# A macaron block in fp32: both feed-forward parts as seven products of halves, in an up phase and a down phase

## The chip, the cores and the metric

The kernel runs on one core of a Trainium2 chip. The metric is the device time of one execution in microseconds. TensorE (PE) does the matrix products and the transposes, VectorE (DVE) and ScalarE (ACT) the element-wise work, GpSimd (POOL) a few row operations, and the SP queue issues nearly all DMAs. Every engine works through its own list of instructions in a fixed order; an instruction that waits holds back all that stand behind it on its engine.

## The reference

All in float32, one sequence of 1024 tokens, model width 1024, feed-forward width 2816.

```python
def swiglu(x, w1, w3, w2):
    return (jax.nn.silu(x @ w1) * (x @ w3)) @ w2
...
        x = layer_norm(ALPHA * x + 0.5 * swiglu(x, ffn1_w1[i], ffn1_w3[i], ffn1_w2[i]),
                       ln1_g[i], ln1_b[i])
        proj = x @ w_in[i]
        q_lat, kv_lat, k_rope, u, g_a, g_b = jnp.split(proj, SPLIT_POINTS, axis=-1)
        y_a = mla_attention(q_lat, kv_lat, k_rope, q_norm_g[i], kv_norm_g[i],
                            w_uq[i], w_uk[i], w_uv[i]) @ w_o_attn[i]
...
        merged = jax.nn.sigmoid(g_a) * y_a + jax.nn.sigmoid(g_b) * y_b
```

After that come the out projection and its layer norm, a second feed-forward part of the same form with its layer norm, and a gated projection of a side input. A second block, a mixer whose norm is modulated by a row computed with `mod_w`, ends the program; the change does not touch its products.

## The kernel before

Each float32 operand is held as the exact sum of a high and a low part (type `fp32r`), so each product of tiles is three matmuls of 128 x 128 by 128 x 512 (`mm3`, line L100). The parts are made by `split`: ScalarE casts the high part (L79), VectorE subtracts it (L80).

`ffn` (L169 to L219) goes over the 22 feature tiles of 128 in blocks of two, the last two blocks of three. For each feature tile and token half it forms the two up products (24 matmuls each), then `silu` (L201), the product (L202) and the split into `hh` and `hl`. Then the block's part of the down product goes into the eight token tiles `acc`, which lie in SBUF all along; VectorE adds each PSUM result to them (L215 to L219). Weights come from HBM once, block by block, and nothing of the hidden layer leaves the chip. In matmuls, one feed-forward part has 22 x 2 x 2 x 24 = 2112 up and 22 x 16 x 3 = 1056 down.

Two pieces of work that need no result of the feed-forward part run beside it. Beside the first it is `s5_tables`, a generator whose pieces are emitted by `tick`: the tables of the state-space branch, complex products on VectorE in a scratch tile `arena`, with transposes on TensorE and round trips through DRAM (`sd`). Beside the second it is `modulation` (multiply-adds L1214, 70 instructions of VectorE). The order of instructions on each engine is fixed when the program is built. Buffers come from pools; a pool's space is given to the next pool once its last reader is done, and the first writer into it waits for that.

After the first feed-forward part come `latents`, `u_cols`, and sixteen `gates` columns (48 matmuls a column each); between them stand eight `s5_batch` (chunk scans that read a batch's tables, `s5b_tab`), one for every two gates. After a feed-forward part the layer norm of its token tiles runs as a chain of small instructions (`nq`, L106 to L131); POOL applies gain and bias to the rows (`affine`, L1027 and L1028).

## Time and profile before

| | before |
|---|---|
| time, median of 3 runs | 3319.93 us (3316.15 to 3321.29) |
| span of the profiled execution | 3318.2 us |
| granted TensorE clock, mean | 0.992 |
| PE busy | 3244.3 us (98%) |
| DVE busy | 2046.8 us (62%) |
| ACT busy | 1103.9 us (33%) |
| POOL busy | 147.9 us (4%) |
| moved by DMA | 293.51 MB, mean 88 GB/s |

The profiled execution lies inside the range of the three runs, so its microseconds can be compared with the median as they are. The first feed-forward part lies at 0 to about 780 us, latents, gates and attention at about 800 to 1480 us, the second feed-forward part at about 1660 to 2400 us.

### The profile page before, as it was taken

To read this page: it belongs to the slowest core of one execution; us is meant where nothing else is said; L and a number is where in the kernel's file an instruction comes from. 1 tells how busy PE (TensorE), PEld (TensorE's weight loads), DVE (VectorE), ACT (ScalarE), POOL (GpSimd) and SP (SyncE) were. 2 spreads that over 40 slices of the span, in tenths; PEclk is the share of its full clock that TensorE was granted. 3 is DMA by queue.
4 is the path that set the end of the run, shared out by engine and by line. 5 is a ranking of instruction groups with operands and counts; after the bars stand their busy time and mean duration, and the time that the engine had idled before them with its cause. 6 is when DMAs were issued, how large, how long until landed. Compare 5 with 4: busy or idle time off the path is not lost.

```text
span 3318.2 us, 38245 instructions
## 1 busy us (share of the span) xinstructions
PE 3244.3 (98%) x15029; PEld 2638.8 (80%) x15029; DVE 2046.8 (62%) x3446; ACT 1103.9 (33%) x1579; POOL 147.9 (4%) x86
## 2 busy tenths in 40 slices
PE   9999999997999999999999999999989999999998
PEld 7878878876888888877778888888868888888786
DVE  6755555447236577776664543332498498899668
ACT  3111111123221266652331111122144456555443
POOL 0000000002200000000230000000040000000000
PEclk9999999998999999999999999999989999999999
DMA  4222222221434300034322232111123222322545
GB/s 131 61 69 73 71 79 63 73 80 45 138 122 140 114 16 13 14 127 145 132 80 76 74 99 69 45 57 51 45 89 118 91 76 76 97 85 72 195 156 182
DMA packets 291971, 293.51 MB, mean 88 GB/s; under 512 B 42581, under 2 KB 228366, under 8 KB 290766
## 3 DMA queue, kind: packets, MB, share of 16 engines
q1 hardware_dynamic: 291790, 291.06, 27.9%
q8 instruction: 118, 1.93, 0.2%
q14 instruction: 63, 0.52, 0.0%
HBM read 234.90 MB, written 56.10 MB: 88 GB/s over the span
## 4 chain that ended last, share of the span: by engine, by line
PE 91%; DVE 5%; DMA 2%; ACT 2%; issue 1%; SPq 0%; DVEq 0%; ACTq 0%
PE up L100 56%; PE dn L100 19%; PE up L1018 10%; PE tr L858 1%; PE dn L875 1%; DVE x L80 1%; DVE wl L80 1%; PE tr L143 1%; DVE sm L841 0%; PE up L544 0%; DMA gb<-gd 0%; DMA y<-yd 0%; DMA raw<-in_ffn_w_dram 0%; DVE nq L113 0%; ACT e L845 0%
## 5 line engine op out<-in xcount | busy, mean ns | idle before, releaser
L100 PE MATMUL up<-x,wh 128*128 128x512 f32 x5088 | 1640.1, 397 | 28.6 <-DVE x L80 22.5
L100 PEld LDWEIGHTS up<-x,wh 128*128 128x128 f32 x5088 | 955.5, 188 | 262.7 <-DVE x L80 25.9
L100 PE MATMUL up<-x,wl 128*128 128x512 f32 x2544 | 1006.8, 396 | 0.4 <-DVE wl L80 0.3
L100 PEld LDWEIGHTS up<-x,wl 128*128 128x128 f32 x2544 | 478.6, 188 | 114.0 <-DVE wl L80 1.4
L80 DVE TENSOR_TENSOR wl<-raw,wh 128x1024 fp32r<-128x1024 f32 (+3 forms) x251 | 316.9, 1264 | 273.5 <-ACT wh L79 271.0
L79 ACT CAST wh<-raw 128x1024 fp32r<-128x1024 f32 (+3 forms) x251 | 254.0, 1014 | 454.3 <-PE up L100 290.9
L1018 PE MATMUL up<-wh,x 128*128 128x512 f32 x1024 | 322.3, 396 | 0.0
L100 PE MATMUL dn<-w2l,hh 128*128 128x512 f32 x640 | 253.6, 397 | 0.0
L100 PE MATMUL dn<-w2h,hh 128*128 128x512 f32 x640 | 251.1, 393 | 0.0
L100 PE MATMUL dn<-w2h,hl 128*128 128x512 f32 x640 | 250.8, 392 | 0.0
L215 DVE SCALAR_TENSOR_TENSOR acc<-dn,acc 128x512 f32<-128x512 f32 x160 | 109.7, 689 | 212.0 <-PE dn L100 211.8
L201 ACT ACTIVATE s<-up 128x512 f32<-128x512 f32 x88 | 52.5, 597 | 564.4 <-PE up L100 564.2
L1018 PEld LDWEIGHTS up<-wh,x 128*128 128x128 f32 x1024 | 193.5, 190 | 41.4 <-issue 0.2
L1018 PE MATMUL up<-wl,x 128*128 128x512 f32 x512 | 202.9, 398 | 4.7 <-ACT xf L1769 2.4
L219 DVE TENSOR_TENSOR acc<-acc,dn 128x512 f32<-128x512 f32 x144 | 98.5, 684 | 134.0 <-PE dn L100 133.2
L202 DVE TENSOR_TENSOR s<-s,up 128x512 f32<-128x512 f32 x88 | 60.3, 685 | 186.1 <-ACT s L201 186.1
L1690 DVE SCALAR_TENSOR_TENSOR cv<-u,kc,cv 128x1024 f32<-128x1024 f32 x120 | 153.2, 1276 | 1.2
L100 PEld LDWEIGHTS dn<-w2l,hh 128*128 128x128 f32 x640 | 120.2, 188 | 28.8 <-issue 0.5
L100 PEld LDWEIGHTS dn<-w2h,hh 128*128 128x128 f32 x640 | 120.1, 188 | 27.7
L100 PEld LDWEIGHTS dn<-w2h,hl 128*128 128x128 f32 x640 | 120.2, 188 | 27.0
L1018 PEld LDWEIGHTS up<-wl,x 128*128 128x128 f32 x512 | 97.1, 190 | 29.7 <-DVE wl L80 3.1
L100 PE MATMUL up<-k,qh 128*128 128x512 f32 x256 | 92.9, 405 | 2.3 <-ACT e L845 2.3
(515 smaller groups left out, 4016.3 us busy)
## 6 DMA issues: line engine op xcount, KB each, us to landing
raw<-in_ffn_w_dram SPq DMA_DIRECT2D x132, 512.0 KB
raw<-in_w_in_dram SPq DMA_DIRECT2D x69, 512.0 KB
raw<-in_w_out_dram SPq DMA_DIRECT2D x44, 512.0 KB
s5b_tab<-sd SPq DMA_DIRECT2D x8, 1792.0 KB
sd<-arena SPq DMA_DIRECT2D x48, 256.0 KB
raw<-in_mod_w_dram SPq DMA_DIRECT2D x24, 512.0 KB
gd<-g SPq DMA_DIRECT2D x16, 512.0 KB
gb<-gd SPq DMA_DIRECT2D x16, 512.0 KB
```

Source lines behind the costliest of these rows:

```text
L79: (copy or nc.scalar.copy)(hi, x)
L80: nc.vector.tensor_tensor(out=lo, in0=x, in1=hi.bitcast(F32), op=ALU.subtract)
L100: nc.tensor.matmul(out, lhsT=a, rhs=b, start=i == 0, stop=i == n - 1)
L143: nc.tensor.transpose(t[:, j * P:(j + 1) * P], tiles[j][:, k * P:(k + 1) * P], self.ident)
L201: nc.scalar.activation(out=s, in_=p1, func=AF.Silu)
L202: nc.vector.tensor_tensor(out=s, in0=s, in1=p3, op=ALU.mult)
L215: nc.vector.scalar_tensor_tensor(out=x, in0=o, scalar=0.5, in1=x, op0=ALU.mult, op1=ALU.add)
L219: nc.vector.tensor_tensor(out=x, in0=x, in1=o, op=ALU.add)
L858: nc.tensor.transpose(t[:, i * P:(i + 1) * P], e[:, c], self.ident)
L875: nc.tensor.matmul(po[:, :256], lhsT=w, rhs=pt[i][:, kt], start=kt == 0 and i == 1, stop=kt == 7 and i == 0)
L1018: self.nc.tensor.matmul(o, lhsT=a, rhs=b[:, c], start=k == 0 and m == 0, stop=k == K - 1 and m == 2)
L1690: v.scalar_tensor_tensor(out=st["y"], in0=u[:, j:j + S], scalar=k, in1=st["y"], op0=ALU.mult, op1=ALU.add)
```

## The change

Both feed-forward parts are computed with seven products of halves where there were eight. In the up phase a pair of feature tiles, the two token halves and the two halves of the 1024 inputs make the 2 x 2 scheme: `x0` to `x6` are sums and differences of quarters of the input, made once (`first_half`, `second_half`), and for each pair VectorE forms the sums of weight tiles and the sums of the products. The results of each pair are combined once more, four as float32 (`hf`) and three as high and low parts (`hs`), and written to DRAM through the SP queue. Then the down phase runs seven `product`s of 132 matmuls: a quarter of w2 is held on chip in a `V` tile, VectorE adds quarters to each other in place and splits them, and the hidden operand comes back from DRAM. Matmuls of one part: 11 x 168 = 1848 up (two pairs have 48 of theirs taken ahead in `up_lead`), 7 x 132 = 924 down.

Moved with it: `modulation` is emitted in pieces beside both up phases; `s5_tables` stands beside `latents`, `u_cols` and gates 0 to 4, and gates from there on take their tiles from a pool that replaces the tables' pool; the `s5_batch`es stand one per gate after gates 6 to 13; the token rows of the second feed-forward part go to DRAM (`xd2`) before it and come back in its down phase, where POOL's affine is applied to them; the layer norm after a feed-forward part is done per half, tiles 0 to 3 before the last product is emitted, 4 to 7 behind it.

```diff
+    def mm12(self, out, w, ks, x, start, stop):
...
+        for kx, k in enumerate(ks):
+            for a, b in ((0, 1), (1, 0), (0, 0)):
+                nc.tensor.matmul(out, lhsT=w[a][:, k], rhs=x[b][:, kx], start=start and i == 0, stop=stop and i == 11)
...
+        wa = None if lead else self.split(r0)
...
+        v.tensor_tensor(out=S[:, U], in0=r1[:, L], in1=r1[:, U], op=ALU.add)
+        v.tensor_tensor(out=S[:, L], in0=S[:, U], in1=r0[:, L], op=ALU.add)
+        wb = self.split(S)
...
+        v.tensor_tensor(out=r1[:, L], in0=r1[:, L], in1=r0[:, L], op=ALU.add)
+        wc = self.split(r1)
...
+        v.tensor_tensor(out=o[1, 0], in0=b, in1=o[0, 1], op=ALU.add)
+        v.tensor_tensor(out=o[0, 1], in0=c, in1=o[0, 1], op=ALU.subtract)
+        v.tensor_tensor(out=o[1, 1], in0=o[1, 0], in1=c, op=ALU.subtract)
...
+            put(0, s[0, 0])
+            put2(2, s[1, 1])
...
+    def ffn_down(self, fp, vr, acc, w2, hd, scale, load, half):
...
+                if add:
+                    plus(V[k][:, ps], V[add][:, ps])
...
+                self.split(V[k][:, ps], hi=z[:, 0, :n], lo=z[:, 1, :n])
+                if i < 4:
+                    h = self.split(self.raw(hf[i, :, ps], [P, n, HALF]))
+                else:
+                    h = [self.stream.tile([P, n, HALF], F32R, tag=tg, bufs=3, name=self.uid("h")) for tg in ("wh", "wl")]
+                    for e in range(2):
+                        nc.sync.dma_start(h[e].bitcast(F32), hs[i - 4, :, u, e, :n])
...
+        loads((0, 1))
+        for t in range(8):
+            load(t)
...
+        half(0)
+        p = even()
+        product(6, (1, 0), p)
+        for t in range(4):
+            plus(acc[4 + t][:, lo], p[t])
+        half(1)
...
+            if i < 5:
+                tick()
+            if i == 4:
+                tick(999)
+                tabs.close()
+                s5.append(tabs.enter_context(self.pool("s5")))
+                got.append(self.s5_load(0, s5[0], sd, ud))
+            if 6 <= i < 14:
+                batch()
...
+                    for u in (t - 1, t):
+                        nc.sync.dma_start(xd2[u], acc[u])
```

Three places of the order that is fixed when the program is built follow; the numbers in the names are running numbers of buffers, and what an instruction waits for stands in brackets.

TensorE, the change, from the last matmul of gate 6 (`up_983`) to the first of gate 7 (`up_1003`); `tr_...<-ident,arena` and L715, L716 are transposes and products of the tables, L768 and L802 the first batch.

```order
L100 MATMUL up_983_7361<-x_767_4843,wh_981_7357 128x512
L715 MATMUL tr_939_6801<-arena_5473 64x128 [waits DVE_49,Activation_49]
...
L693 MATMUL tr_950_6940<-ident_69,arena_5473 128x128 [waits DVE_49,Activation_49]
...
L693 MATMUL tr_963_7106<-ident_69,arena_5473 128x128 [waits DVE_49,Activation_49]
...
L693 MATMUL tr_970_7209<-ident_69,arena_5473 128x128 [waits DVE_49,PE_49]
...
L802 MATMUL dn_998_7473<-s5b_U_974_7272,s5b_tab_973_7270 128x128
L100 MATMUL up_1003_7502<-x_766_4842,wh_1001_7498 128x512 [waits Activation_49]
```

Before, TensorE had between two gates at this place only the ones-products of the norm and the first batch:

```order
L713 MATMUL tr_683_6418<-ones_74,sq_682_6416 128x1 [waits Activation_49]
...
L100 MATMUL up_687_6434<-x_4_87,wh_685_6430 128x512
...
L544 MATMUL up_693_6499<-s5b_U_676_6349,s5b_tab_675_6347 128x128 x7
L578 MATMUL dn_701_6538<-s5b_U_676_6349,s5b_tab_675_6347 128x128
...
L100 MATMUL up_708_6579<-x_3_86,wh_706_6575 128x512 [waits Activation_49]
```

What moved: the products of the last three and a half table batches stand between two gates, where all tables had been done far ahead.

VectorE, the change, from the end of the first up phase to the first split for the down phase: `t`, `s` and `g` are results of the last pair, `sp` what is written to DRAM as parts, `wl_618` and `wl_622` hidden operands for later units, `v_611` the first part of w2.

```order
L299 TENSOR_TENSOR t_574_3456<-up_583_3520,t_574_3456 128x512 [waits PE_49]
L80 TENSOR_TENSOR wl_622_3702<-raw_620_3699,wh_621_3701 128x1024 [waits DMAHW0_49,Activation_49]
L80 TENSOR_TENSOR sp_587_3572<-s_555_3327,sp_587_3572 128x512 [waits DMAHW4_49,Activation_49]
L305 TENSOR_TENSOR s_553_3325<-s_553_3325,t_574_3456 128x512 [waits DVE_49]
L327 TENSOR_TENSOR g_588_3576<-s_553_3325,s_555_3327 128x512 [waits DMAHW3_49,DVE_49]
L329 TENSOR_TENSOR g_589_3577<-g_588_3576,s11_560_3370 128x512 [waits DMAHW6_49,DVE_49]
L331 TENSOR_TENSOR s_553_3325<-s11_560_3370,s_553_3325 128x512
L80 TENSOR_TENSOR sp_590_3581<-g_589_3577,sp_590_3581 128x512 [waits DMAHW5_49,Activation_49]
L334 TENSOR_TENSOR g_589_3577<-g_589_3577,s_554_3326 128x512 [waits DVE_49]
L80 TENSOR_TENSOR sp_591_3586<-s_553_3325,sp_591_3586 128x512 [waits DMAHW5_49,Activation_49]
L80 TENSOR_TENSOR v_611_3630<-V_606_3619,v_611_3630 128x1024 [waits DMAHW3_49,Activation_49]
```

Before, there was no such border; the parts of the weights of a block stood ahead of the block's last products:

```order
L80 TENSOR_TENSOR w2l_266_2581<-raw_264_2578,w2h_265_2580 128x1024 [waits Activation_49]
L80 TENSOR_TENSOR w2l_269_2587<-raw_267_2584,w2h_268_2586 128x1024 [waits DMAHW5_49,Activation_49]
L202 TENSOR_TENSOR s_260_2483<-s_260_2483,up_259_2434 128x512 [waits Activation_49]
L80 TENSOR_TENSOR hl_254_2319<-s_260_2483,hh_253_2318 128x512 [waits Activation_49]
L80 TENSOR_TENSOR wl_295_2774<-raw_293_2771,wh_294_2773 128x1024 [waits DMAHW4_49,Activation_49]
```

What moved: ten instructions stand between the last result of the up phase and the first part of w2.

VectorE, the change, in the second feed-forward part's down phase, at the border of products 0 and 1: `acc` are token rows that came back from DRAM and through POOL, `V_2513` and `v_2555` the operand from w2.

```order
L80 TENSOR_TENSOR v_2551_16790<-V_2513_16545,v_2551_16790 128x1024 [waits Activation_49]
L80 TENSOR_TENSOR wl_2558_16830<-raw_2556_16827,wh_2557_16829 128x1024 [waits DMAHW6_49,Activation_49]
L399 TENSOR_TENSOR acc_2501_16525<-acc_2501_16525,up_2516_16548 128x512 [waits Activation_49,Pool_49]
L363 TENSOR_TENSOR V_2513_16545<-V_2513_16545,V_2514_16546 128x1024 [waits DVE_49]
L399 TENSOR_TENSOR acc_2503_16527<-acc_2503_16527,up_2517_16549 128x512 [waits Activation_49,Pool_49]
L80 TENSOR_TENSOR v_2555_16824<-V_2513_16545,v_2555_16824 128x1024 [waits Activation_49]
```

Before, VectorE's waits for POOL in the second part stood at its first additions (L215), with the weights' parts ahead of them:

```order
L80 TENSOR_TENSOR w2l_1687_12768<-raw_1685_12765,w2h_1686_12767 128x1024 [waits DMAHW6_49,Activation_49]
L80 TENSOR_TENSOR hl_1661_12472<-s_1681_12754,hh_1660_12471 128x512 [waits Activation_49]
L215 SCALAR_TENSOR_TENSOR acc_1539_11717<-dn_1688_12771,acc_1539_11717 128x512 [waits PE_49,Pool_49]
```

What moved: POOL's sixteen row operations and the waits for them went from the start of the part into its down phase, where the splits of the next product stand behind them.

## Rows read from the trace of the kernel before

**Rows 1.** The page: span, busy times, and the chain that ended last by line.

```profile
span 3318.2 us, 38245 instructions
...
PE 3244.3 (98%) x15029; PEld 2638.8 (80%) x15029; DVE 2046.8 (62%) x3446; ACT 1103.9 (33%) x1579; POOL 147.9 (4%) x86
...
PE up L100 56%; PE dn L100 19%; PE up L1018 10%; PE tr L858 1%; PE dn L875 1%; DVE x L80 1%; DVE wl L80 1%; PE tr L143 1%; DVE sm L841 0%; PE up L544 0%; DMA gb<-gd 0%; DMA y<-yd 0%; DMA raw<-in_ffn_w_dram 0%; DVE nq L113 0%; ACT e L845 0%
```

**Rows 2.** Longest pieces of that chain: start, duration, what, how many.

```profile
833.44 112.46 PE up L100 x482
...
1560.82 22.25 PE up L1018 x96
```

**Rows 3.** Busy time of each engine in stretches of the span.

```profile
60.00:700.00 640.00, 640.00 (x2835) 512.58 (x2834) 361.08 (x774) 113.39 (x164) 0.00 (x0) 1.00 0.24 69
700.00:815.00 115.00, 96.23 (x424) 77.46 (x423) 71.78 (x124) 34.17 (x42) 18.89 (x8) 0.93 0.22 70
815.00:960.00 145.00, 144.64 (x657) 117.72 (x655) 40.34 (x49) 34.83 (x45) 22.76 (x8) 0.99 0.34 108
960.00:1140.00 180.00, 180.00 (x952) 152.14 (x952) 105.02 (x190) 35.22 (x43) 0.00 (x0) 1.00 0.45 143
...
1640.00:2380.00 740.00, 732.55 (x3203) 591.73 (x3202) 325.93 (x468) 144.32 (x199) 46.49 (x16) 1.00 0.24 69
...
2440.00:2580.00 140.00, 138.45 (x643) 113.96 (x643) 121.57 (x318) 62.09 (x87) 29.18 (x10) 0.98 0.37 123
2580.00:3110.00 530.00, 527.53 (x2331) 426.09 (x2330) 424.42 (x498) 280.65 (x349) 0.00 (x0) 1.00 0.27 85
```

**Rows 4.** VectorE's groups at 60 to 700 us, by shape.

```profile
L219 DVE TENSOR_TENSOR acc<-acc,dn 128x512 f32<-128x512 f32 x127 | 86.8, 684 | 130.6 <-PE dn L100 129.8
L80 DVE TENSOR_TENSOR wl<-raw,wh 128x1024 fp32r<-128x1024 f32 x35 | 42.8, 1223 | 45.0 <-ACT wh L79 45.0
...
L80 DVE TENSOR_TENSOR hl<-s,hh 128x512 fp32r<-128x512 f32 x35 | 24.1, 687 | 4.3 <-ACT hh L79 4.1
...
L243 DVE TENSOR_TENSOR s<-arena 128x512 f32<-128x512 f32 x24 | 19.9, 830 | 0.1
...
L248 DVE TENSOR_TENSOR arena<-s,s 128x512 f32<-128x512 f32 x24 | 16.6, 690 | 23.3 <-DMA sd<-arena 12.3 <-PE tr L469 8.8 <-PE tr L491 1.9
L250 DVE TENSOR_TENSOR arena<-arena,s 128x512 f32<-128x512 f32 x24 | 16.3, 681 | 0.0
...
L243 DVE TENSOR_TENSOR arena<-arena 128x64 f32<-128x64 f32 x19 | 4.2, 220 | 1.5 <-DMA arena<-in_ssm_b_re_b_dram 1.2
```

**Rows 5.** The modulation's line: duration minimum, median, maximum, first and last start.

```profile
L1214 DVE SCALAR_TENSOR_TENSOR am<-raw,sil,am x70: 739/746/753, 1667.9 to 2040.9; 128x512 f32<-128x512 f32 x70
```

**Rows 6.** TensorE's waits at 700 to 815 us: total, times, longest.

```profile
PE up L100 <- DVE x L80: 18.8, 3, 16.6
```

**Rows 7.** Timeline at the first feed-forward part's end: VectorE, then POOL.

```profile
792.79 0.16 DVE L112 SCALAR_TENSOR_TENSOR nq<-nq 128x2 f32<-128x2 f32 x1
792.98 2.34 DVE L113 SCALAR_TENSOR_TENSOR nq<-nq 128x2 f32<-128x2 f32 x1
...
792.95 9.24 POOL L1027 TENSOR_TENSOR acc<-acc,arena 128x1024 f32<-128x1024 f32 x4 [792.51 <-DVE nq L112]
```

**Rows 8.** Timeline at the second part's start: VectorE, then POOL.

```profile
1644.23 3.42 DVE L80 TENSOR_TENSOR wl<-raw,wh 128x1024 fp32r<-128x1024 f32 x1
...
1652.68 1.22 DVE L80 TENSOR_TENSOR w2l<-raw,w2h 128x1024 fp32r<-128x1024 f32 x1 [2.21 <-ACT w2h L79]
...
1641.35 11.39 POOL L1027 TENSOR_TENSOR acc<-acc,bg 128x1024 f32<-128x1024 f32 x4 [281.05 <-PE tr L143]
```

**Rows 9.** Stretches of 4 and 5 us in which the DMA engines were full.

```profile
12.00:16.00 4.00, 4.00 (x23) 3.28 (x22) 1.49 (x3) 1.18 (x2) 0.00 (x0) 1.00 1.08 356
...
990.00:995.00 5.00, 5.00 (x27) 4.19 (x27) 0.17 (x1) 0.00 (x0) 0.00 (x0) 1.00 1.00 358
```

**Rows 10.** The cast that a split starts with, ScalarE at 60 to 700 us.

```profile
L79 ACT CAST wh<-raw 128x1024 fp32r<-128x1024 f32 x36 | 37.6, 1046 | 116.0 <-PE up L100 113.4 <-DMA raw<-in_ffn_w_dram 2.6
```

More of the change, by code (lines that the diff above doesn't have):

```diff
@@ L1100, in block1, with half @@
-            self.u_cols(0, X, fp, "w2h", ud)
+            X = []
+            def half(h):
+                if h == 0:
+                    xp = R.enter_context(self.pool("x", side="right"))
+                    X.extend(self.new_xT(xp))
+                for t in range(h * 4, h * 4 + 4):
+                    self.norm_stage(acc, t, X, "ln1_g", "ln1_b", fp, keep, eps=4 * LN_EPS)
+            self.ffn_down(fp, ExitStack(), acc, w2, hd, 2 * ALPHA, load, half)
+            self.u_cols(0, X, fp, "uc", ud)
@@ L1104, in block1, with tick, batch, step @@
         nc.sync.dma_start(self.rt[64:128], I["k_rope"])
-        with self.pool("s5") as sp:
-            lat, kr = self.latents(X, ap, sp)
-            self.u_cols(2, X, sp, "g", ud)
-            rms = self.rms_latents(lat, sp)
-            got = [self.s5_load(0, sp, sd, ud)]
-            def step(i):
-                b = i // 2
-                if i == 1 or i and i % 2 == 0:
-                    if b < 7:
-                        got.append(self.s5_load(b + 1, sp, sd, ud))
-                    self.s5_batch(b, sp, *got.pop(0), zd)
-                if rms:
-                    rms.pop(0)()
-            self.gates(X, sp, gd, step)
+        tabs = ExitStack()
+        tp = tabs.enter_context(self.pool("tabs"))
+        tables = self.s5_tables(tp, sd)
+        def tick(n=8):
+            for _ in range(n):
+                next(tables, None)
+        lat, kr = self.latents(X, ap, tp, tick)
+        self.u_cols(2, X, tp, "g", ud)
+        tick()
+        rms = self.rms_latents(lat, tp)
+        s5 = []
+        got = []
+        nb = [0]
+        def batch():
+            b = nb[0]
+            nb[0] += 1
+            if b < 7:
+                got.append(self.s5_load(b + 1, s5[0], sd, ud))
+            self.s5_batch(b, s5[0], *got.pop(0), zd)
+        def step(i):
+            if rms and i < 10:
+                rms.pop(0)(s5[0] if s5 else tp)
+            if i < 5:
+                tick()
+            if i == 4:
[5 more added lines that the diff above has]
+                batch()
+        self.gates(X, lambda: s5[0] if s5 else tp, gd, step)
+        tabs.close()
         R.close()
@@ L1142, in block1 @@
+        q1.close()
+        with self.pool("ep") as ep:
+            mods = self.modulation(ep)
+            self.ffn_up(w1, w3, xc, eq, ep, hd, leads, lambda: mods and mods.pop(0)())
+            while mods:
+                mods.pop(0)()
+        xa.close()
+        q0.close()
         self.lates = ExitStack()
@@ new lines, in part, with begin, finish @@
+            return [lambda k=k: two(k) for k in range(0, KD, 2)] + [end]
+        def begin():
+            v.memset(onem, 1.0)
+            for e, nm in enumerate(("c_2", "c_ctx_2")):
+                nc.scalar.activation(out=sil[:, e], in_=self.vec[nm], func=AF.Silu)
+        def finish():
+            for e in range(2):
+                v.scalar_tensor_tensor(out=mod[:, e, 1], in0=mod[:, e, 1], scalar=1.0, in1=self.vec["norm_g_2"],
+                                       op0=ALU.add, op1=ALU.mult)
+            self.lru_consts(self.const, pool)
@@ L1266, in context @@
                                   f.rearrange("p (k c) -> p k c", k=4))
-        return step
+        parts = [part(b, h) for b in range(3) for h in range(2)]
+        if not again:
+            return [begin] + sum(parts[:3], [])
+        return [begin] + sum(parts[3:], []) + [finish] + [lambda t=t: context(t) for t in range(2)]
     def row_rms(self, x, junk):
```

517 lines of the change are left out of this document (372 added, 145 removed).

## The prediction

> **What bounds the kernel now.** I read the page first. TensorE is busy 98% of the span, and matmul lines make up most of the chain that ended last: 56% up, 19% down in the feed-forward parts [rows 1]. So a matmul that goes away should give back its pitch, as long as nothing else takes its place. The pitch comes from the long pieces of that chain: 112.46 us for 482 matmuls is 0.2333 us each, 22.25 us for 96 is 0.2318 us [rows 2] (the busy mean of a matmul is no price, since matmuls overlap).
>
> The stretches come next, because an average over the span hides what each stage has to spare [rows 3]. Inside the first feed-forward part TensorE is never idle (640.00 of 640) and VectorE has 361.08 us of work, part of it the tables. From 815 to 1140 us VectorE has only 145.36 us of work in 325. Two stretches show what the two engines do side by side when VectorE is nearly full: 87% busy at 2440 to 2580 us with TensorE at 138.45 of 140, and 80% at 2580 to 3110 with 527.53 of 530. So a VectorE at 80% need not cost TensorE anything.
>
> **What goes.** Each part loses 2112 - 1848 = 264 up and 1056 - 924 = 132 down matmuls; two parts lose 792. At 0.2333 us that is **-184.8 us** (-183.6 at the other pitch). All else below is what the seven-product form asks of the other engines.
>
> **Steady up phase.** A pair of feature tiles is 168 matmuls, 39.2 us. VectorE has for it, from the code: per half three splits of 1024 (1.22 us), one of 512 (0.69), four weight sums and seven reads of PSUM (0.69 and 0.68); per pair eleven more instructions of 512 (four products, three splits for DRAM, four sums). With the durations of [rows 4] this is 31.3 us, 80%; the addition rows [rows 4] stand for the sums. At that share [rows 3] showed no loss. What is tight is one place in each half: the split of `wc` waits for ScalarE's cast (1.05 us, [rows 10]) and its own buffer, with 2.8 us of matmuls to hide behind. I take 8 us over 44 halves, bounds 0 and 30.
>
> **Modulation and the pairs with a lead.** 70 multiply-adds of 0.746 us [rows 5], 52 us, go beside the up phases, some 6 us a pair while they last. In most pairs 39.2 us hide 37. The first two pairs of each part have only 120 matmuls, 28 us, against some 33 us of VectorE: 5 us a pair at most. I take 8 us, bounds 0 and 20.
>
> **Starts of the parts.** The five combined operands of the second half cost 36 instructions of 512, 25 us, and the 96 matmuls taken ahead give 22 us of cover, part of which needs the first of these operands. I take 8 us for each part, 16 together; bounds 0 and 40.
>
> **Borders of the phases.** The order shows ten instructions of VectorE between the last result of the up phase and the first part of w2. By [rows 4] they and that split take 8.6 us, with the cast some 10 to 11, and TensorE has nothing else to do: **22 us** for two parts, bounds 10 and 40. At the same place SP's queue carries four quarters of w2 (2.9 MB each), 4.2 MB of token rows and 1 MB of gain and bias rows ahead of the hidden operand of product 1. About 20 MB at 357 GB/s, the rate of full DMA engines [rows 9], are 55 us. Against that stand the last 12 us of the up phase (the first quarter of w2 takes the place of an operand last read there), the 10 us above and product 0's 31 us. I take 7 us in all, bounds 0 and 40.
>
> **POOL in the second down phase.** Sixteen row operations go from the part's start to its products 0 and 1. Their price is read from the neighbours: at 792.79 us an `nq` instruction of two elements takes 0.16 us, the next, started together with POOL's operation, 2.34 us, as long as one of POOL's four (9.24 / 4 = 2.31 us) [rows 7]. At the second part's start a split that takes 1.22 us alone takes 3.42 us under POOL [rows 8]. So each of POOL's operations can hold VectorE up by one of its own length: 16 x 2.31 = 37 us. Product 0 has 28 us of VectorE work for 31 us of matmuls, product 1 about 24, so some 10 us are spare, and the start of the part gets some relief. I take 20 us, bounds 5 and 45.
>
> The Trainium skill's page "SBUF — State Buffer" (section "Who interferes with whom") says that a VectorE instruction with two SBUF inputs and a GpSimd instruction that reads SBUF exclude each other, and that the loser is blocked for the whole instruction. The rows agree. By that rule taken strictly, with no slack, the term is 37 us and the sum 17 us higher.
>
> **The tables, beside latents and gates.** This is the largest term. Their cost on VectorE is read where they run now: six groups of 24 instructions of 512 elements, 112.2 us together (first and last of them in [rows 4]), six of 19 instructions of 64 elements at 4.1 to 4.2 us each, and some 30 us of smaller ones: about 168 us. They also wait 23.3 us ahead of one line for DMA and TensorE [rows 4]. Now they stand behind the first part, where latents, `u_cols` and gates 0 to 6 give 15 columns of 48 matmuls, 168 us. The end of the part adds some 18 us. Against these 186 us VectorE has the tables' 168, some 25 of the norms and reads at the part's end, and the splits and evacuations of the 15 columns, about 30: 223, and 20 or so of waits on DRAM trips: some 243. The order puts gate 7 behind the last table product, so TensorE must stand for the difference: **55 us**, bounds 25 (no wait is exposed, instructions overlap a little) and 90 (all of them are).
>
> After that one batch goes with each gate. From its list of instructions at the durations of [rows 4] I estimate 14 us of VectorE, against 15 of TensorE: 5 us, bounds 0 and 15.
>
> **Ends.** At the first part's end TensorE waits 18.8 us now [rows 6], and eight `nq` instructions stand under POOL there [rows 7]. With the norm of tiles 0 to 3 done beside product 6, POOL is done earlier: -5 us over both parts, bounds -15 and 10. **Clock.** The stretch with that wait has a granted clock of 0.93, those with a full TensorE 1.00 [rows 3]; the new bubbles of 10 to 55 us should each leave some microseconds at the lower level of 1.2 GHz. I take 8 us, bounds 0 and 20.
>
> **Sum.** 8 + 8 + 16 + 22 + 7 + 20 + 55 + 5 - 5 + 8 = 144 us given back of 184.8. 3318.2 - 184.8 + 144 = 3277; the median stands 1.7 us above the span, so **3279 us**.
>
> **Rivals.** (a) TensorE stays the bound nearly everywhere. For it: [rows 3], where a VectorE at 80 to 87% costs nothing, and prefetch by three buffers. Against it: the table products stand in TensorE's own order ahead of gate 7. With the tables at their lower bound 25, the borders at 22 and 20 for all else it gives 3318.2 - 184.8 + 67 + 1.7 = 3202 us.
>
> (b) Slower, by one mechanism: the tables are a serial chain, not a load. They hold one batch in `arena` at a time; its complex products, DRAM trips, transposes and copies depend on each other. Where they run now this is not seen, because pieces are spread over 640 us. If a batch takes 25 us from end to end, eight take 200, with the parameters' part (some 40) and the 43 us at the end of the part ahead of them 283 against 186: a stall of 97 us instead of 55, and the gain is gone from there on (55 + 41 is the point at which the sum equals the old time). At 30 us a batch the stall is 137 and the time some 3361.
>
> (c) The borders' DMA isn't hidden: the quarters of w2 are only asked for when the up phase ends, because SP stands behind the spills. Then 55 us stand against 41, 14 us more in each part, and the sum is 3279 + 28 = 3307. For it: SP issues in order, and the last spills wait for VectorE. Against it: the first quarter's issue stands ahead of most of them.
>
> That the matmuls do not fall away is no rival: they are counted in TensorE's order.
>
> **Chances.** Forecast 0.45 (its own range 3245 to 3312), (a) 0.25, (b) 0.17, (c) 0.13. A run of this kernel can be told from the old one by about 0.2%, 6.6 us: below 3313 is faster, above 3327 slower. Faster: 0.43 + 0.25 + 0.08 = 0.76; slower: 0.12 of (b), 0.03 of (c) and 0.01, 0.16; the rest, 0.08, the same. For 8 in 10 the range must take in most of (a) and part of (b): 3190 to 3335.
>
> **What the changed profile would show.** TensorE's busy time lower by about 185 us; in the up phases TensorE at 95% or more with VectorE near 80%; two idle stretches of about 10 us at the phase borders, whose releaser is a split of w2; in the second down phase VectorE instructions of 3.4 us beside POOL and idle TensorE in products 0 and 1; and one long wait on a table product ahead of gate 7. The forecast is wrong if VectorE is the releaser all through the up phases, if the wait ahead of gate 7 is under 25 or over 90 us, or if a DMA is the releaser for tens of microseconds in products 0 and 1.

## The result, and the profile after

The changed kernel takes 3371.57 us (median of four runs, 3370.34 to 3374.5); the kernel before, on the same chip, 3320.61. The ratio is 1.0155, 95% interval [1.0140, 1.0169]: it is 51 us slower. The forecast was 3279 us, the range 3190 to 3335.

The head of the page of the changed kernel: busy time by engine, and the granted clock in 40 slices.

```profile
span 3369.4 us, 38690 instructions
...
PE 3114.4 (92%) x14237; PEld 2521.5 (75%) x14237; DVE 2477.0 (74%) x4049; ACT 1309.7 (39%) x1839; POOL 152.0 (5%) x86
...
PE   7999978989983999999989999949989999999998
...
PEclk8999989999976999999999999979999999999999
```

TensorE was busy 98% of the span [rows 1] and is now busy 92%. Its idle time went from 73.9 to 255.0 us. Its busy time fell by 129.9 us, though the matmuls that are gone are worth more (189.4 us, by the first experiment below): those that are left were slower. The slices with a low clock are among those with idle time.

The stretches of the changed kernel (busy time of each engine, then granted clock, DMA share and GB/s), which answer to [rows 3]:

```profile
0.00:100.00 100.00, 76.27 (x331) 59.11 (x332) 75.36 (x119) 45.08 (x72) 0.20 (x4) 0.91 0.46 144
100.00:450.00 350.00, 349.75 (x1524) 281.70 (x1523) 279.71 (x411) 113.68 (x152) 0.00 (x0) 1.00 0.43 139
450.00:550.00 100.00, 73.17 (x295) 58.12 (x294) 58.67 (x65) 30.25 (x37) 0.00 (x0) 0.86 0.68 248
700.00:800.00 100.00, 88.40 (x385) 69.75 (x385) 62.66 (x88) 34.29 (x45) 44.81 (x16) 0.93 0.33 110
...
900.00:1100.00 200.00, 125.43 (x593) 102.57 (x592) 131.90 (x293) 35.18 (x52) 0.00 (x0) 0.73 0.40 123
1100.00:1200.00 100.00, 92.49 (x504) 78.83 (x503) 80.98 (x138) 17.86 (x23) 0.00 (x0) 0.98 0.56 183
1740.00:1800.00 60.00, 43.80 (x189) 34.48 (x188) 56.52 (x111) 27.80 (x44) 0.00 (x0) 0.86 0.33 98
1800.00:2150.00 350.00, 348.74 (x1506) 279.24 (x1505) 273.66 (x427) 122.66 (x176) 0.00 (x0) 1.00 0.45 145
2150.00:2300.00 150.00, 102.38 (x381) 79.70 (x381) 109.91 (x91) 39.24 (x48) 49.84 (x16) 0.82 0.57 205
2420.00:2560.00 140.00, 127.03 (x582) 103.02 (x582) 100.36 (x167) 53.94 (x67) 44.63 (x16) 0.96 0.35 116
```

The two up phases (100 to 450, 1800 to 2150) run as forecast: VectorE at about 80%, TensorE never short of work. The time is lost at the seams: 23.7 us idle at the start of the first part (before: 7.3 in the same 100 us), 26.8 at its phase border, 82.1 from 900 to 1200 where the tables now stand, 16.2 at the start of the second part, 47.6 at its border and the products behind it. Before, 815 to 1140 us had hardly any idle time [rows 3].

TensorE's longest waits in the changed kernel (total, times, longest):

```profile
PE up L385 <- DVE v L80: 74.3, 12, 18.7
PE tr L693 <- DVE arena L472: 39.8, 6, 11.3
PE up L768 <- DMA s5b_U<-ud: 26.9, 4, 21.2
PE up L175 <- ACT wh L79: 22.7, 4, 15.5
```

The first is the phase borders and the first products of the down phases (`v` is a split piece of w2), the second the tables, the third mostly the load of the first batch behind them, the fourth mostly the start of the second part. All waits on table products (L693, L715, L716) add up to 52.2 us.

**The clock** shows at each of these seams. The timeline of the changed kernel on TensorE, at the first matmuls behind the 15.5 us wait at the second part's start (start, duration of one):

```profile
1768.83 0.79 PE L175 MATMUL up<-x4l,wh 128*128 128x512 f32 x1 [15.49 <-ACT wh L79]
...
1773.36 0.63 PE L175 MATMUL up<-x4h,wl 128*128 128x512 f32 x1
1773.79 0.63 PE L175 MATMUL up<-x4h,wh 128*128 128x512 f32 x1
...
1774.57 0.40 PE L175 MATMUL up<-x4h,wl 128*128 128x512 f32 x1
1774.81 0.39 PE L175 MATMUL up<-x4h,wh 128*128 128x512 f32 x1
```

Up to 1774.2 the matmuls start 0.43 us apart, from then on 0.23: after the wait TensorE runs at 1.2 GHz for 5.4 us (granted clock 0.50 from 1769 to 1774), and then at 2.4 (1.00 from 1775 to 1780).

### The profile page after: what moved, and what is told of

It is laid out like the page before. It is cut to its first block, busy times and chain, and to the rows that moved or that the text cites. A ratio compares the mean times of both kernels' runs of the same rounds, so it can differ in the third digit from the quotient of the medians.

```text
span 3369.4 us, 38690 instructions
## 1 busy us (share of the span) xinstructions
PE 3114.4 (92%) x14237; PEld 2521.5 (75%) x14237; DVE 2477.0 (74%) x4049; ACT 1309.7 (39%) x1839; POOL 152.0 (5%) x86
## 5 line engine op out<-in xcount | busy, mean ns | idle before, releaser
L100 PE MATMUL up<-x,wh 128*128 128x512 f32 x2336 | 751.0, 399 | 11.5 <-DVE acc L363 4.8
L100 PEld LDWEIGHTS up<-x,wh 128*128 128x128 f32 x2336 | 441.0, 189 | 121.2 <-issue 5.7
L100 PE MATMUL up<-x,wl 128*128 128x512 f32 x1168 | 464.3, 398 | 0.4 <-DVE wl L80 0.4
L100 PEld LDWEIGHTS up<-x,wl 128*128 128x128 f32 x1168 | 221.1, 189 | 53.0 <-DVE wl L80 0.8
L80 DVE TENSOR_TENSOR v<-V,v 128x1024 fp32r<-128x1024 f32 x84 | 105.2, 1254 | 141.6 <-ACT v L79 141.6
L385 PE MATMUL up<-v,wh 128*128 128x512 f32 x352 | 124.0, 430 | 73.1 <-DVE v L80 73.1
L79 ACT CAST v<-V 128x1024 fp32r<-128x1024 f32 x84 | 81.9, 978 | 265.6 <-PE up L385 150.8
L385 PE MATMUL up<-v,h 128*128 128x512 f32 x528 | 127.8, 399 | 1.2 <-DVE v L80 1.2
L385 PEld LDWEIGHTS up<-v,h 128*128 128x128 f32 x528 | 98.2, 188 | 25.1 <-DVE v L80 2.4
L80 DVE TENSOR_TENSOR pl<-tr,ph 128x512 fp32r<-128x512 f32 x128 | 85.7, 683 | 10.6 <-ACT ph L79 10.2
```

Source lines behind the costliest of these rows:

```text
L79: (copy or nc.scalar.copy)(hi, x)
L80: nc.vector.tensor_tensor(out=lo, in0=x, in1=hi.bitcast(F32), op=ALU.subtract)
L100: nc.tensor.matmul(out, lhsT=a, rhs=b, start=i == 0, stop=i == n - 1)
L385: nc.tensor.matmul(out[t], lhsT=h[a][:, kk, tk], rhs=z[:, b, kk], start=u + kk + m == 0, stop=p0 + kk == NP - 1 and m == 2)
```

## Experiments

Differences are to the changed kernel's 3371.6 us unless said otherwise. The kernel before, run beside each group, lay between 3318.7 and 3321.0, so differences under 3 us aren't read.

**1. What the matmuls are worth.** The kernel before, with as many matmuls left out as the change removes (the last of the eight input tiles in each up product, the last token tile in the down products):

```diff
-  ... for k in range(KD)])
+  ... for k in range(KD - 1)])        # both up products
...
-                for n in range(2):
+                for n in range(2 if t < 7 else 0):
```

> The kernel before with 792 matmuls of its feed-forward parts left out (the last of the eight input tiles in every up product, and the whole down product of the last token tile), so its output is not the reference's; everything else of the old form stays. If a matmul that goes away gives back its pitch, the time is 3320.6 - 184.8 = 3136 us (3125 to 3150). If the old form's VectorE or its loads are nearly the bound already, part of it is not given back: 3160 us or more.

Measured: 3131.25 us (two runs), 189.4 less. Its page, span and TensorE:

```profile
span 3129.1 us, 36625 instructions
...
PE 3065.3 (98%) x14237; PEld 2494.4 (80%) x14237; DVE 2014.9 (64%) x3406; ACT 1105.8 (35%) x1579; POOL 153.7 (5%) x86
```

It has as many matmul records as the changed kernel (14237), so the two can be set side by side: the changed kernel's span is 240.3 us longer, of which 255.0 - 63.8 = 191.2 us are idle time and 3114.4 - 3065.3 = 49.1 us are slower matmuls. That is what the change gives back: 240, where the forecast had 144.

How much of the 49.1 us is the clock can be bounded. All stretches with a granted clock of 0.50 taken together, in the changed kernel and then in this one:

```profile
sum 263.70, PE 113.62 PEld 91.12 DVE 176.85 ACT 52.60 POOL 43.06; mean PE 5.41 PEld 4.34 DVE 8.42 ACT 2.50 POOL 2.05
sum 52.15, PE 37.37 PEld 28.31 DVE 40.85 ACT 23.94 POOL 20.47; mean PE 4.67 PEld 3.54 DVE 5.11 ACT 2.99 POOL 2.56
```

TensorE worked 76.3 us more at the lower of its two levels. The same work takes at least half as long at the higher one, so the clock cost at most 38 us; for 11 us or more of the 49.1 no run shows the cause.

**2. POOL in the second down phase.** The scale and offset of the eight token rows, sixteen POOL instructions, are left out:

```diff
                 nc.sync.dma_start(acc[t], xd2[t])
-                self.affine(acc[t], gb[2], nc.gpsimd)
```

> The change, with POOL's sixteen row operations of the second down phase left out (gain and bias of the residual there are not applied). Theory 1, POOL holds VectorE up: products 0 and 1 of that phase, idle for 47 us now and at a low clock, shorten to what the first part's down phase shows; 35 to 45 us less, some 3331 us. Rival, the loads at the border are the wait and POOL only stands beside it: 10 us less or nothing, 3360 us or more.

Measured: 3346.4 us, -25: between the two. Timelines of the changed kernel, VectorE and then POOL, during the second down phase's product 1:

```profile
2235.38 3.27 DVE L363 TENSOR_TENSOR V<-V,V 128x1024 f32<-128x1024 f32 x1
2238.58 3.36 DVE L80 TENSOR_TENSOR v<-V,v 128x1024 fp32r<-128x1024 f32 x1
```

```profile
2234.22 6.63 POOL L1253 TENSOR_TENSOR acc<-acc,bg 128x1024 f32<-128x1024 f32 x2
```

And VectorE at the same place without the POOL instructions:

```profile
2226.26 1.22 DVE L80 TENSOR_TENSOR v<-V,v 128x1024 fp32r<-128x1024 f32 x1
...
2228.53 2.48 DVE L363 TENSOR_TENSOR V<-V,V 128x1024 f32<-128x1024 f32 x2
```

The two engines take turns, one instruction each in 3.3 us, and a VectorE instruction lasts 3.3 us where it lasts 1.2 alone. That agrees with the rule of the Trainium skill's page "SBUF — State Buffer" (section "Who interferes with whom") that the two exclude each other. Its strict price, 37 us, is not reached; that part of the delay falls where VectorE had slack is likely, but not shown.

**3. The tables: a load?** The 512-wide complex products of the tables are done on half of their elements (the other half of the tables is left out):

```diff
+        nc.gpsimd.memset(arena, 0.0)
...
+                lo = lambda zs: [z[:, :GB // 2] for z in zs]
+                return self.cmul_parts(lo([v4(z) for z in o]), lo(pw), lo(cf), lo([v4(z) for z in s4]))
```

> The change, with the complex products of 512 elements in the tables done on half of their elements (the tables' other half is zero), the same instructions, trips and transposes in the same order. Theory 1, VectorE's load is what gates wait for: 24 x 6 instructions lose about 0.33 us each, 47 us less, some 3325 us. Rival, the chain of trips and hand-overs sets it (waits on DRAM, transposes, the pool's hand-over): less than 25 us, 3347 us or more.

Measured: 3357.6 us, -14. VectorE's six groups of table products (24 instructions each) fell from 111.0 to 67.0 us. If VectorE's work set the time, these 44 us would have gone. The load theory falls here.

**4. The tables: a chain?** A second scratch, so that odd batches of tables don't wait until the even batch has left `arena`:

```diff
+        arena2 = pool.tile([P, 5632 - 2240], F32, name="arena2")
...
+            at = at0 if b % 2 == 0 else at1
-            s4 = [pool.tile([P, N], F32, tag="tf", bufs=2, name=self.uid("s4")) for _ in range(2)]
+            s4 = [pool.tile([P, N], F32, tag="tf", bufs=4, name=self.uid("s4")) for _ in range(2)]
```

> The change, with a second scratch tile, so that every other table batch has its own and two batches can be on their way at once; the same instructions and bytes. Theory 1, the tables are a serial chain (22 to 25 us from one batch to the next ahead of gate 7, VectorE busy 38 of 50 us): 25 to 45 us less, 3327 to 3347 us. Rival, VectorE's load sets the pace: 8 us less or nothing.

Measured: 3335.9 us (3330.3 to 3337.6), -35.6. The work and the engines are the same, only the scratch (with its two helper tiles `s4`) is doubled. The timeline of the changed kernel on TensorE shows it batch by batch:

```profile
996.43 1.08 PE L693 MATMUL tr<-ident,arena 128*128 128x128 f32 x4 [10.40 <-DVE arena L472]
1021.37 1.09 PE L693 MATMUL tr<-ident,arena 128*128 128x128 f32 x4 [10.47 <-DVE arena L472]
1043.47 1.09 PE L693 MATMUL tr<-ident,arena 128*128 128x128 f32 x4 [11.35 <-DVE arena L472]
```

The same transpose of consecutive batches comes 24.9 and 22.1 us apart, each behind a wait of over 10 us. VectorE has only 131.90 us of work in the 200 from 900 to 1100: it waits for DMA and for TensorE in turn, on the same `arena`. Two of its waits there (the longest of all, 21.4 us, is for the first batch behind the tables):

```profile
DVE arena L472 <- DMA sd<-arena: 17.2, 6, 4.3
DVE arena L472 <- PE tr L715: 16.7, 7, 5.2
```

So 35.6 us, their share of the clock included, were this chain. With two scratches the stretch from 900 to 1200 us has 244.70 us of TensorE work instead of 217.9, at a clock of 0.89; 55 us of it are still idle.

**5. The hand-over behind the tables.** A small pool of its own holds the gates' tiles and the first batch's tables, so that the first load doesn't wait for the tables' pool to close:

```diff
-                got.append(self.s5_load(0, s5[0], sd, ud))
+                got.append(self.s5_load(0, pre, sd, ud, 1))
...
-        self.gates(X, lambda: s5[0] if s5 else tp, gd, step)
+        self.gates(X, lambda: pre, gd, step)
```

> The change, with the gates' tiles and the first batch's table and inputs in a small pool of their own, so that gate 7 and batch 0 stand ahead of the last tables and batch 0's inputs are loaded early (a batch's output takes another tile's place to make room). Theory 1, the hand-over of the pool is a cost of its own: the wait of 21.2 us for the inputs of batch 0 goes, 15 to 25 us less, 3347 to 3357 us. Rival, the wait only moves to the next batches, since the chain of tables ends no earlier: 5 us less or nothing.

Measured: 3419.0 us, +47. The theory gets no support, but the edit brought waits of its own (the batches' results share a buffer, and VectorE waits 32.8 us for their writes to DRAM). TensorE's waits for the load of `U` are 67.5 us in all. The longest of them (20.3, before 21.2) is still there. What the hand-over costs by itself stays open.

**6. Which part costs?** The first part, tables and gates as in the kernel before, only the second part by seven products (with the whole modulation beside its up phase):

```diff
-            self.ffn_down(fp, ExitStack(), acc, w2, hd, 2 * ALPHA, load, half)
+            self.ffn(fp, X, acc, I["ffn1_w1"][0], I["ffn1_w3"][0], I["ffn1_w2"][0],
...
-            return [begin] + sum(parts[:3], [])
```

> Only the second feed-forward part by seven products, the first one as before with the tables beside it, latents and gates as before, the whole modulation beside the second up phase. Theory 1, the costs are local (gates about 107 us with their clock, the first part's border 34, its start 24): 3371.6 + 92.4 - 165 and some 8 for the modulation, about 3307 us. Rival, the costs are spread over both parts alike (VectorE and transfers busier everywhere): half of the change, about 3346 us.

Measured: 3319.8 us, ratio to the kernel before 1.0001 [0.9992, 1.0011]. So the second part gives back all that its 396 matmuls bring (92.4 us at 0.2333), and the 51 us of the slowdown belong to the first part and the tables that it pushed out. The two parts' starts and borders in this kernel:

```profile
1640.00:1700.00 60.00, 43.81 (x197) 34.86 (x196) 52.78 (x109) 36.55 (x53) 0.00 (x0) 0.85 0.40 123
1700.00:2120.00 420.00, 417.94 (x1814) 335.66 (x1814) 351.48 (x558) 131.42 (x178) 0.00 (x0) 1.00 0.47 151
2120.00:2330.00 210.00, 158.87 (x616) 122.75 (x615) 138.50 (x124) 64.22 (x83) 50.69 (x16) 0.86 0.54 187
```

Even with all of the modulation the up phase loses 2 us in 420. Start and border lose 16 and 51.

**7. The borders: SP's queue, the row loads, the spill buffers.** Three edits of the changed kernel. First, the first three quarters of w2 are asked for from POOL's queue:

```diff
+        for k in ((0, 0), (0, 1), (1, 1)):
+            loads(k, nc.gpsimd)
```

> The change, with the loads of the first three quarters of w2 issued from POOL's queue in place of SP's. Theory 1, SP's order is the wait at the border of the phases (the first quarter was issued at 475.45 us, behind loads that waited for VectorE, though its place was free about 11 us earlier): the idle stretches of 17 and 9 us in the first part and their like in the second shrink, 15 to 30 us less, 3342 to 3357 us. Rival, the DMA engines' rate is the limit there (390 to 410 GB/s from 480 to 530 us): 5 us less or nothing.

Measured: 3362.0 us, -9.6, between the two. Second, the token rows are asked for only when product 0 is done, and added after product 2:

```diff
-        for t in range(8):
-            load(t)
...
         loads((1, 1))
+        for t in range(8):
+            nc.scalar.copy(acc[t][:, 0:1], s1[t % 4][:, 0:1])
+            load(t)
```

> The change, with the token rows of the down phases loaded (and in the second part put through POOL) only once product 0 is done, and added after product 2. Theory 1, the rows' 4.2 MB and POOL's operations stand in the way of products 0 and 1: 10 to 25 us less, 3347 to 3362 us. Rival, they hold up VectorE just as long one product later: no change within 6 us.

Measured: 3370.7 us, no change, as the rival has it. In the first part the stretch from 450 to 550 us stays as it was (73.40 us of TensorE work, 73.17 without the edit), so the loads of the rows hold up nothing there. In the second part 2150 to 2300 us gain 7.7 us of work and 2300 to 2560 lose 5.3: POOL's operations only come later (2254 to 2304 us). Third, the spill buffers. The timeline of the changed kernel at the first border (SPq is SP issuing DMAs; the last up matmul starts at 475.66):

```profile
482.93 0.38 SPq L323 DMA_DIRECT2D hs<-sp  x1
...
487.26 3.65 SPq L360 DMA_DIRECT2D V<-in_ffn_w_dram  x4
491.87 0.37 SPq L323 DMA_DIRECT2D hs<-sp  x1
491.91 0.62 ACT L79 CAST sp<-s 128x512 fp32r<-128x512 f32 x1 [8.92 <-DMA hs<-sp]
492.44 1.99 ACT L79 CAST v<-V 128x1024 fp32r<-128x1024 f32 x2
...
494.79 0.79 PE L385 MATMUL up<-v,wh 128*128 128x512 f32 x1 [18.74 <-DVE v L80]
```

ScalarE's last spill cast needs one of two spill buffers. The DMA that empties it was issued at 482.93, among the loads of w2, and the buffer is free 9 us later. The first cast of w2 (`v`) stands behind that in ScalarE's order, and VectorE and TensorE behind the cast. Two edits give the last spills another buffer: two of the weight sums' (`S`), or one of the weight splits' (`wl`):

```diff
+                if p == NF // 2 - 1 and i != 2:
+                    z = ep.tile([P, KD, P], F32, tag="S", bufs=2, name=self.uid("S"))
```

```diff
+                if p == NF // 2 - 1 and i == 1:
+                    z = self.stream.tile([P, 2, HALF], F32R, tag="wl", bufs=3, name=self.uid("sp"))
```

> The changed kernel, where in the last pair of each up phase two of the three spills of split operands take a buffer of the weight sums in place of the pair of spill buffers. If the border is held by ScalarE's wait for a spill buffer (8.9 us at the first border, the first cast of w2 stands behind it), each border gets some 8 us shorter: -12 to -18, 3354 to 3360. Rival: the first pieces of w2 land hardly sooner than that, so the wait only changes its name: -4 at most, 3367 to 3372.

> The changed kernel, where only the very last spill of split operands of an up phase takes a buffer of the stream of weight splits, which the down phase uses again from its fourth piece on. If ScalarE's wait for a spill buffer (8.9 us at the first border, 2.9 at the second) holds the first product, 8 to 12 us go: 3360 to 3364. Rival: the first pieces of w2 or the memory under the first split tile are free no sooner: within 4 us of 3371.6.

Measured: 3377.6 and 3374.8 us, +6 and +3 (the latter hardly more than the noise). In the second, the cast of `v` does come early, at 480 us, but now VectorE waits for the buffer that the spill took, from the timeline of this run:

```profile
487.33 1.70 SPq L326 DMA_DIRECT2D hs<-sp  x2
...
499.75 1.23 DVE L80 TENSOR_TENSOR wl<-raw,wh 128x1024 fp32r<-128x1024 f32 x1 [16.03 <-DMA hs<-sp]
```

The wait has only changed hands. In these traces the last spills, 0.5 MB each, land 9 to 12 us after their issue, among 2.9 MB quarters of w2, and whoever needs their memory next waits; no run took that away. The page "DMA: Bandwidth & Descriptors" of the Trainium skill (section "Queues, rings and completion order") says that each DMA engine takes the descriptors of one ring in order. With w2 on the same queue as the spills that would make them wait as they do here. With w2 on POOL's queue, the first edit of this group, the spill takes longer still: issued at 480.03, it holds its buffer until 493.78, and the first product waits 20.9 us where it waited 18.7. So the order in the ring is at least not the whole cause. The DMA engines are full in both runs, which fits the rival of the first edit: share 1.03 and 403 GB/s with w2 on POOL's queue (480 to 510 us), and in the changed kernel:

```profile
480.00:530.00 50.00, 27.12 (x97) 21.44 (x98) 25.57 (x26) 10.59 (x12) 0.00 (x0) 0.73 1.04 399
```

The changed kernel's timeline shows one more wait at each border, ahead of product 1, for which no run was made:

```profile
511.14 1.06 ACT L162 ACTIVATE bg<-bg 128x1024 f32<-128x1024 f32 x1 [16.72 <-DMA bg<-in_ln_g_dram]
...
515.78 0.80 PE L385 MATMUL up<-v,wh 128*128 128x512 f32 x1 [8.09 <-DVE v L80]
...
2222.57 1.06 ACT L162 ACTIVATE bg<-bg 128x1024 f32<-128x1024 f32 x1 [23.55 <-DMA bg<-in_ln_g_dram]
...
2228.75 0.79 PE L385 MATMUL up<-v,wh 128*128 128x512 f32 x1 [15.55 <-DVE v L80]
```

ScalarE scales the gain row (`bg`), and the first casts for product 1 stand behind that in its order. SP asks for the row behind w2, at 501.97 and 2212.62, and it lands 9 to 10 us later. With w2 on POOL's queue SP asks for it at 495.57 and 2199.39; ScalarE's wait for it falls to 11.24 and 4.47 us, while its wait for the last spill's buffer grows from 8.92 to 11.08 and from 2.89 to 8.75. By these traces what the first edit won comes from the gain row rather than from the spills; no run moved the row alone.

**8. Do the gains add up?** The changed kernel with the second scratch, w2 from POOL's queue, and the row instructions of experiment 2 on VectorE instead of POOL:

```diff
-                self.affine(acc[t], gb[2], nc.gpsimd)
+                self.affine(acc[t], gb[2], nc.vector)
```

> The changed kernel with three edits together: the second scratch for every other batch of tables (-35.6 us alone), the first three quarters of w2 asked for from POOL's queue (-9.5 alone), and the affine of the second down phase on VectorE in place of POOL (leaving it out gave 25; 16 instructions on VectorE give back 20 at most where no slack is left, so -5 to -15). If the losses are separate waits in separate places, they add up: -50 to -60, 3311 to 3322 us, level with the kernel before. Rival: the queue and the affine mend the same wait at the border of the second part, so only the larger counts: -40 to -47, 3325 to 3332.

Measured: 3311.5 us, ratio to the kernel before 0.9975 [0.9964, 0.9986]; -60. That is below the rival's 3325 to 3332, as if the waits were separate ones. With 35.6 and 9.6 for the first two, 15 are left for the third, the upper end of what was expected of it; the third was not run alone.

**9. A better second part.** From the hybrid of experiment 6 (3319.8 us): its border has 16.6 us of waiting for a context row, the last piece of the modulation. First, the modulation beside the gates, alone and with the other two edits of experiment 8:

```diff
+            mods = self.modulation(sp)
             def step(i):
+                for _ in range(2):
+                    if mods:
+                        mods.pop(0)()
```

> The hybrid (first part as before, second by seven products) with the modulation moved from the second up phase to the gates, where VectorE has 170 of 300 us of work. If the border of the second part loses because the last pieces of the modulation (16.6 us waited for a context row) stand between up phase and down phase on TensorE and on SP's queue, the time falls by 10 to 25 us from the hybrid's 3319.8: 3295 to 3310. Rival: the up phase hides the modulation wholly (417.9 of 420 us busy there) and the border waits for w2 and the POOL-held VectorE anyway: within 5 us, 3315 to 3322.

> The same hybrid with two more edits: the first three quarters of w2 from POOL's queue and the affine of the second down phase on VectorE. If the border's idle time (51 us in the hybrid) is the sum of the context piece, the queue and the exclusion by POOL, 10 to 25 us more than the run beside it go: 3275 to 3297, clearly faster than the kernel before (3313 is the point). Rival: the chain last sum, cast, split, product remains and the row instructions on VectorE stand in its way: at most 8 us more, 3295 to 3312.

Measured: 3341.1 us, 21 more than the hybrid, and 3318.0 with the two edits. The theory on the context row falls; the two edits bring their 23 us, but from a worse start. Among the gates the modulation's pieces stand in the way of the batches (the stretch from 1100 to 1200 us falls from 94.79 to 81.67 us of TensorE work), and at the border the wait for `v` only grew, in this run:

```profile
PE up L440 <- DVE v L80: 42.7, 7, 14.6
```

where the hybrid had 23.0: with the context row gone TensorE came to the next wait earlier. So the two edits on the hybrid itself, with the modulation where it was:

> The hybrid (first part as before, second by seven products, modulation beside the second up phase) with the first three quarters of w2 asked for from POOL's queue and the affine of the second down phase on VectorE. With the modulation among the gates these two edits gave 23 us (3341.1 to 3318.0). If what they mend is a wait of the border that doesn't depend on where the modulation stands, the time is 3319.8 - 23 = 3297, 3290 to 3303, faster than every kernel here. Rival: here the last context piece stands at the border too (16.6 us waited) and covers what the queue costs, so only the affine counts: -10 to -14, 3306 to 3310.

Measured: 3298.8 us, 0.9943 [0.9930, 0.9957], as expected. Now TensorE's longest wait is the context row:

```profile
PE tr L1606 <- ACT raw L1600: 23.2, 1, 23.2
```

Then the modulation's pieces two at a time in the middle of the up phase, so that the context rows are done before the border, first with the spill buffers `S` of experiment 7, then without them:

```diff
+                for _ in range(2 if 9 <= ticks[0] < 17 else 1):
```

> The hybrid with two mends (3298.8 us) and two edits more: the spill buffers as in the run beside it, and the pieces of the modulation taken two at a time in the middle of the up phase, so that the context pieces are done some eight places earlier and don't stand between the phases. If the 23.2 us that TensorE waits there for a context row are a wait of their own, 15 to 25 us go: 3274 to 3284. Rival: behind the context rows the first product would wait for w2 and its split as well: -3 to -10, 3289 to 3296.

> The hybrid with two mends (3298.8 us), and the pieces of the modulation taken two at a time in the middle of the up phase as the one edit more. If the 23.2 us that TensorE waited for a context row between the phases are a wait of their own, and the run before hid it behind 19 us for its spill buffers: 3276 to 3284. Rival: the split of w2 comes no sooner than the context row did: 3292 to 3299.

Measured: 3295.5 with other spill buffers, as the rival has it, and 3285.7 us without, just above the expected range, the latter 0.9895 [0.9880, 0.9910]: faster than the two kernels by 34 and 86 us. The first of the two shows the spills once more: `v` takes the memory of `S`, and its cast waits for the spill to land, in the timeline of that run:

```profile
2130.52 0.97 SPq L382 DMA_DIRECT2D hs<-S  x2
...
2149.50 1.99 ACT L79 CAST v<-V 128x1024 fp32r<-128x1024 f32 x2 [19.13 <-DMA hs<-S]
```

Of the 23.2 us of the context row 13 were won: 16.9 us of waiting for `v` came up behind it.

## Why the prediction was wrong

| step | forecast, us | shown, us |
|---|---|---|
| matmuls gone | -184.8 | -189.4 (experiment 1) |
| up phases, modulation, pairs with a lead | +16 | 1.5 idle in 700 |
| starts | +16 | 16.4 more idle in the first part, 16.2 idle in the second (before: 7.45 in the whole part) |
| first part's border and its DMA | +14.5 (half of 22 + 7) | 26.8 idle, 450 to 550 |
| second part's border, and POOL | +34.5 (other half + 20) | 47.6 idle, of it POOL 25 (experiment 2, with its share of the clock) |
| tables and batches beside latents and gates | +60 | 82.1 idle, 900 to 1200, of it 52.2 for tables and 26.9 for the batches' loads |
| ends | -5 | 7.2 less idle in the first part, 2.4 more in the second |
| clock | +8 | at most 38 of 49.1 us of slower matmuls (experiment 1) |

The idle times are read from the stretches after, against [rows 3] where before had some; for the second part's end, 12.97 us idle after, the stretch before is this one, with 10.56:

```profile
2380.00:2580.00 200.00, 189.44 (x871) 154.20 (x871) 175.24 (x421) 83.69 (x114) 46.24 (x16) 0.96 0.30 99
```

Three steps failed: the clock, the tables with what follows them, and the borders. Together they make up most of the 96 us by which 240 exceeds 144.

**The clock step was mis-sized**, 8 us where up to 38 were shown. The forecast took "some microseconds at the lower level" once per bubble and counted few bubbles. Here the seams leave their stretches at 0.73 to 0.98, and where waits follow each other closely TensorE stays at 1.2 GHz between them. In the changed kernel, the stretch in which the last tables are made:

```profile
1000.00:1050.00 50.00, 19.11 (x79) 15.07 (x78) 37.65 (x86) 5.81 (x11) 0.00 (x0) 0.50 0.28 87
```

The granted clock is 0.50 all through, with 19.11 us of work in 50. So idle time costs more than itself. By experiment 1, 191.2 us of it came with 49.1 us of slower matmuls, a quarter, of which the clock is 38 at most.

**The table step failed in its mechanism**, though 82 lies within its bounds. The forecast added up VectorE's work, 243 us against 186 of cover, and took 55 (the difference is 57). Halving the work gave 14 us, giving the chain a second scratch 35.6: it is in large part rival (b), a batch every 22 to 25 us where the rival assumed 25. The 82 us lie between the forecast's 60 and the rival's 97 + 5; with the clock on top they are enough to take the gain. That the waits on table products alone, 52.2 us, come near the 55 is luck. What the forecast left out is the load of the first batch behind the last table: 21.2 us of waiting at once, 26.9 with the other batches, where 5 were set for all that follows the tables.

**The borders were mis-sized**, 29 for two (with their DMA) against 26.8 at the first alone. The chain of ten instructions was right, and the DMA engines carried more than the 357 GB/s that the forecast gave them (399 at the first border). Missing were two waits of ScalarE for a DMA: for the buffer of the last spill, ahead of the first cast of w2, and for the gain row, ahead of product 1. With them the forecast's own sign of being wrong, a DMA that is waited for in products 0 and 1, came true by way of ScalarE. Rival (c) is right only in part: moving the loads to another queue won 9.6 us, taking the rows out of the way nothing. (Its sum counts the 7 us of the forecast again; 14 us in each part make 3300, not 3307.) **Starts:** the forecast took 8 us for each; VectorE has 56.52 us of work in the 60 us around the second start, and TensorE waits 15.5 us for it and then 5.4 us at the lower clock. This was only read from the trace; no run tried it.

**Right were** the price of a matmul, the up phases (a VectorE at 80% costs TensorE nothing, with all of the modulation 2 us in 420), the ends (-4.8 against -5) and the size of POOL's term. That the second part brings nothing was not foreseen: by the forecast's terms it had 92 less 8, 8, 14.5 and 20, a gain of some 40.

**Still open:** what of the 21 us wait for the first batch's load (`U` and `s5b_tab`) the closing of the tables' pool costs, how the spills at the border could be got out of w2's way, what asking for the gain row earlier would win by itself, and what slows the matmuls by the 11 us or more that the clock doesn't explain.

## What to carry to other kernels

Work that hides well beside a long full stage, in small pieces, may be a chain and not a load: before moving it, hold its end-to-end time per piece, not its busy time, against the new cover, and see whether it holds one buffer from beginning to end. Where a stage writes its results out and the next one reads big weights in, look for the buffer that the last write still holds, for small rows that are asked for behind the weights, and for who stands behind either in an engine's order. And put a surcharge on TensorE's idle time, since the matmuls after a long wait run at half speed for a while: here the slower matmuls came to a quarter of it.

## What the runs showed of the hardware

- After an idle wait of 15.5 us TensorE's matmuls came 0.43 us apart for 5.4 us, then 0.23; with waits of 10 us and pieces of work of a few microseconds in turn it stayed at a granted clock of 0.50 from 1000 to 1050 us.
- A VectorE instruction of 1024 elements beside a busy POOL took 3.27 to 3.38 us, alone 1.22 to 1.24. The sixteen POOL instructions took 49.84 us in the changed kernel, 3.1 each, against 2.31 at [rows 7].
- A 0.5 MB write to DRAM held its buffer for 9 us among loads of w2 on the same queue, and 13.8 and 19 us in two runs with w2 on POOL's queue. The DMA engines moved 393 to 413 GB/s there, at a share of 1.03 to 1.05.
